# A decoder block on one core: forty transfers that add up weight blocks in memory, issued from a_v to projection B instead of in the FFN input stage

## The chip, the cores and the metric

The kernel is one launch on one core of a Trainium2 chip. The metric is the device time of that launch in microseconds (us), shown as the median of several runs. The engines named below are PE (matrix multiply; PEld is its weight load), DVE (vector), ACT (scalar), POOL and SP. SP computes nothing here: it issues most of the DMA transfers. POOL computes a little, and it issues the transfers that add to memory. Each engine works through its instructions in the order of the program. An instruction that waits holds up everything behind it on the same engine.

## The reference, cut to what matters

One layer of a decoder for 512 positions of 1024 channels in float32, followed by a final norm:

```python
h = rms_norm(x, norm1_g) * (1.0 + scale1) + shift1          # scale, shift, gate from silu(c) @ w_ada
z = h @ w_in                                                # a_u | a_v | q | k | v | qi | ki | wi | g_a | g_b
y_a = chunked_gmlp(gelu(a_u), gelu(a_v), ...)
y_b = dsa_attention(q, k, v, qi, ki, wi)                    # top-256 keys by an indexer score
merged = sigmoid(g_a) * (y_a @ w_proj_a) + sigmoid(g_b) * (y_b @ w_proj_b)
x = x + gate1 * (merged @ w_out)
h2 = rms_norm(x, norm2_g) * (1.0 + scale2) + shift2
f_g, f_u = split(h2 @ w_ffn_in)
x = x + gate2 * ((silu(f_g) * f_u) @ w_ffn_out)
return rms_norm(x, final_norm_g)
```

`w_ffn_out` has 2816 x 1024 elements. `w_ada` has 1024 x 6144 elements; its six sections of 1024 columns give shift1, scale1, gate1, shift2, scale2 and gate2.

## The kernel before, in words

**Products.** Each float32 operand is split into a rounded part `hi` and a rest `lo`, and a product is three matmuls: hi x hi, hi x lo, lo x hi (`mm3`, lines 53 to 55). ACT makes `hi` of a weight chunk (line 112). DVE or POOL makes `lo` (line 116).

**Stages.** In the order of the program: the norm and the adaLN numbers; q, k, v and the indexer; a_v (8 weight chunks); a_u (8 chunks); then four times one group of gate A and one of projection A (16 chunks); attention with the gate B products mixed in (19 rounds); projection B (8 chunks); the output projection; the FFN input stage (20 rounds, lines 1590 to 1700, tile `R`); the FFN output stage (tile `pfo`); the final norm.

**Block sums.** The output projection, the FFN input and the FFN output use a Strassen-like scheme: seven products of half-size blocks instead of eight. The weight side of the FFN output needs sums of blocks of `w_ffn_out`. Four such sums, `wsum1` to `wsum4`, are formed in DRAM by DMA alone, five chunks of 256 x 512 elements (512 KB) each. One chunk takes six steps (`wsum_steps`, lines 292 to 314): two copies into wsum1 and wsum3; two accumulating transfers on top of them; a copy wsum1 to wsum2; an accumulation on wsum2; a copy wsum2 to wsum4; an accumulation on wsum4. Plain copies are issued by SP (line 307), accumulating ones by POOL (line 305). That is 20 copies and 20 accumulations. Each step has to wait until the transfers of the chunk's step before it have landed, and the engine that issues it does the waiting. The sums are first read in the FFN output stage (`raw<-wsum`).

**Where the steps stand before.** `wstep()` issues the next step of a list. It is called twice in each of the 20 rounds of the FFN input stage. In the list the chunks 0 and 1 alternate, then 2 and 3; chunk 4 comes last, with an empty entry after each step.

**The other loads of SP.** Weight chunks `raw` (512 KB) go into three rotating buffers. A load is issued in program order by `ensure`, when `room` allows it, and SP then waits until the buffer's last reader is done. Loads of `w_ada` for the later sections ("mods", `mod_sec`, lines 200 to 228) stand in the same list: in the gate A and projection A groups one mod follows each weight chunk. Such a load goes into a single buffer `mraw` (line 205), and DVE adds its rows, times the silu of c, onto `acc` (lines 175 and 177). As there is one buffer, the next `mraw` load is issued only when that sum is done, and the weight load that follows it in the list is issued behind it. Sections 2, 3 and 4 are formed so from the end of a_u to projection B, 24 loads of 512 KB, of which 16 belong to the gate A and projection A groups. Section 5 is formed in rounds 1 to 8 of the FFN input stage (`last_mod`), two loads at a time.

**DVE beside it.** From a_v to the end of projection A DVE also runs the top-k search of the indexer (lines 709 and 713), the mixing of a_u (lines 920 and 922) and the products of projection A with its gate (line 995). At the start of attention it makes `lo` of the first gate B chunks (line 116) and the first softmax (line 1029).

**Names in the code around the change.** `opt_b` runs a group of chunks and calls `post` after each of them; `au_post` is that `post` in a_u, gate A and projection A; the loop over `s in range(NU + 3)` is attention; `o_step` is called once in each chunk of projection B.

Of the kernel before, what the change touches and what calls it, by code (L numbers as in the profile page):

```python
# [28 lines left out]
def block_kernel(ctx: ExitStack, tc: tile.TileContext, x, positions, w_ada, b_ada, w_in,  # L29
# [15 lines left out]
    def f(ap):  # L45
        return ap.bitcast(F32)
# [72 lines left out]
    def ensure(upto):  # L119
        upto = min(upto, len(stream) - 1, st["limit"] - 1)  # L120
        while True:
            for i in range(st["prep"], min(st["prep"] + 16, len(stream), st["limit"])):
                if "raw" in stream[i]:
                    continue
                if room(i):
                    issue(i)
                elif stream[i]["kind"] == "w" or not stream[i]["mid"]:
                    break
            if st["prep"] > upto:
                break  # L130
            prep(st["prep"])
            st["prep"] += 1
# [11 lines left out]
    def get(i, ahead=2):  # L144
        k = wseq.index(i)
        ensure(wseq[min(k + ahead, len(wseq) - 1)])
        return chunk[i]
# [144 lines left out]
    def wsum_steps():  # L292

        def step(c, *moves):
            o = slice(256 * c, 256 * c + 256)

            def fn():
                for n, add, src in moves:
                    if isinstance(src, tuple):
                        k = KZ[src[0]][2 * c] * 128  # L300
                        src = w_ffn_out[k:k + 256, 512 * src[1]:512 * src[1] + 512]
                    else:
                        src = wsum[src][o]
                    if add:
                        P.dma_start(wsum[n][o], src, accum_op=OP.add)  # L305
                    else:
                        SY.dma_start(wsum[n][o], src)
            return fn

        parts = [[step(c, *m) for m in (  # L310
            ((1, 0, (0, 0)), (3, 0, (0, 1))), ((1, 1, (0, 1)), (3, 1, (1, 1))), ((2, 0, 1),), ((2, 1, (1, 1)),),
            ((4, 0, 2),), ((4, 1, (1, 0)),))] for c in range(NZ)]
        return ([fn for c in (0, 2) for two in zip(parts[c], parts[c + 1]) for fn in two] +
                [fn for one in parts[4] for fn in (one, None)])

    wsteps = wsum_steps()

    def wstep():
        fn = wsteps.pop(0) if wsteps else None
        if fn:  # L320
            fn()
    assert next(mm_, None) is None
    sec_done = []
    tick = [0]
# [549 lines left out]
    for g in range(4):  # L874
        pb = [bank2(b, "pav") for b in nbanks()]
        for i in W_AV[g]:
            for fn in VT.get(vs, []):
                fn()
            if iu[1] < 24:
                idx_accs()  # L880
            else:
                run_bg(2.0)
            if vs % 2 == 0 and vs:
                for tk in range(4):
                    V.bn_stats(bst[:, tk, (g - 1) * 6:g * 6], vg[tk // 2][:, tk % 2, (g - 1) * 256:g * 256])
            vs += 1
            hi, lo = get(i)
            for tk in range(4):
                opt_a_mm(pb[tk // 2][:, tk % 2], tk, hi, lo, stream[i]["kts"], hT, 8, tk % 2 == 0)
            idx_mms(3)  # L890
        for b in range(2):
            A.activation(vg[b][:, :, g * 256:(g + 1) * 256], pb[b], AF.Gelu_apprx_tanh)
# [34 lines left out]
    AT = {3: [0], 4: [1, 2], 5: [3], 6: [4], 7: [5], 8: [6], 9: [7]}  # L927

    def au_post():
        for m in AT.get(austep[1], []):  # L930
            mix_mm(m)
        austep[1] += 1
# [152 lines left out]
    def gb_part(n, ahead=2):  # L1085
        for k in range(gbn[0], min(gbn[0] + n, 32)):
            g, kt = divmod(k, 8)
            i = W_GB[g][kt // 4]
            hi, lo = get(i, ahead)
            if k % 2 == 0:  # L1090
                mbank[0] = (7, 1, 0, 7)[g]
                sec_tasks()
            if kt == 0:
                gbp[g] = [bank(b, "pgb") for b in ((0, 1), (7, 0), (1, 7), (0, 1))[g]]
            for m in range(2):
                cc = slice(m * 128, (m + 1) * 128)
                mm3(gbp[g][m], (hi[:, kt % 4, cc], lo[:, kt % 4, cc]), hT[kt], kt == 0, kt == 7)
            if kt == 7:
                for m in range(2):
                    A.activation(gbt[g][:, m], gbp[g][m], AF.Copy)  # L1100
        gbn[0] += n
# [4 lines left out]
    for s in range(NU + 3):  # L1106
        if s >= 3:
            yh, yl, pp = at_pv(s - 3)
            A.activation(yh, pp, AF.Copy)
            V.tensor_sub(yl, pp, f(yh))  # L1110
        if s < NU:
            at_qk(s)
            at_soft_a(s)
            if s == 0:
                pa_last[0]()
                at_split(2)
        if 2 <= s <= NU + 1:
            for o, ol, p in at_T(s - 2):
                A.activation(o, p, AF.Copy)
                V.tensor_sub(ol, p, f(o))  # L1120
        if 1 <= s <= NU:
            at_soft_b(s - 1)
        if s < NU:
            at_exp(s)
        if 0 < s < NU - 2:
            at_split(s + 2)
        gb_part(GBN[s], 2 if s else 1)
    mbank[0] = 6

    for g in range(4):  # L1130
# [73 lines left out]
    def o_step():  # L1204
        for fn in O_STEPS.pop(0):
            fn()

    mbank[0] = 5
    o_issue("B11", "B12", "B22")
# [3 lines left out]
    sec_tasks(True)  # L1213


    ss2 = base.tile([128, 4, 5], F32, name="ss2")
    V.memset(ss2, 0.0)
    V.memset(ss2[:, :, 4:5], EPS)
# [404 lines left out]
    for q in range(-2, NQ):  # L1623
        g, u = 2 + q // 2, q % 2
        d = sd[q]
        s_issue(q + 2)
        pre = s_prep(q + 1)
        half_of = lambda t, e: tuple(v[:, :, e] for v in t)
        S2_, S1_, A12, A22, S4_, S3_ = (half_of(d[k], e) for k in "CBD" for e in range(2))
        R = [bank(k, "R")[:, :256] for k in ((4, 1, 0, 7), (5, 2, 3, 6))[q % 2]]  # L1630
        ps = [ffn[0].tile([128, 256], F32, name="ps", tag="rt", bufs=2) for _ in range(2)]
        if q == NQ - 2:
            for i in W_Z[0, 0][:2]:
                issue(i)
        t0, t1 = slice(0, 256), slice(256, 512)
        if u:
            dst = [gtile(2 * g + m) for m in range(2)]
        else:
            fs[0], fs[1] = t512("fs"), t512("fs")
            dst = fs  # L1640
        cur = dict(fs)

        def out_direct(m, p, u=u, dst=dict(enumerate([dst[0], dst[1]])), cur=cur):
            if u:
                V.tensor_mul(dst[m][:, t0], cur[m][:, t0], p)
            else:
                A.activation(dst[m][:, t0], p, AF.Silu)

        def out_late(m, u=u, dst=dict(enumerate([dst[0], dst[1]])), cur=cur):
            if u:  # L1650
                V.tensor_mul(dst[m][:, t1], dst[m][:, t1], cur[m][:, t1])
            else:
                A.activation(dst[m][:, t1], dst[m][:, t1], AF.Silu)

        pre[0][0]()
        sprod(R[0], d["A"], HB[0, 0], True)
        A.activation(R[1], R[0], AF.Copy)  # L1657
        for fn in pre[0][1:]:
            fn()
        while left:  # L1660
            left.pop(0)()
        if q == NQ - 1:
            issue(W_Z[0, 0][2])
        sprod(R[3], S1_, TB[1], True)
        A.activation(ps[0], R[3], AF.Copy)
        for fn in pre[1]:
            fn()
        sprod(R[1], S2_, TB[2], False)
        wstep()
        A.activation(R[2], R[1], AF.Copy)  # L1670
        pre[2][0]()
        pre[2][1]()
        sprod(R[0], A12, HB[1, 0], False)
        if not u:
            out_direct(0, R[0])
        sprod(R[2], S3_, TB[3], False)
        A.activation(ps[1], R[2], AF.Copy)
        pre[3][0]()
        pre[3][1]()
        if u:  # L1680
            out_direct(0, R[0])
        V.tensor_add(dst[1][:, t1], R[3], ps[1])
        sprod(R[1], S4_, HB[1, 1], False)
        out_late(1)
        V.tensor_add(dst[0][:, t1], R[1], ps[0])
        sprod(R[2], A22, TB[4], False)
        out_late(0)
        left.append(lambda fn=out_direct, p=R[2]: fn(1, p))
        if 1 <= q <= 8:
            last_mod(q - 1)  # L1690
        if q == 9:
            last_gate()
        if q == 10:
            for b_ in (3, 2):
                mbank[0] = b_
                sec_tasks(one=True)
        wstep()
        if q in (9, 13, NQ - 2):
            a_sum("S1", {9: 0, 13: 2}.get(q, 1))
    assert not wsteps  # L1700


    xo = []
# [134 lines left out]
    for tk in range(2):  # L1838
        for z in range(2) if tk else (None,):
            c = ALL if z is None else slice(256 * z, 256 * z + 256)  # L1840
# [66 lines left out]
```

## Time and profile before

| | |
|---|---|
| median of 3 runs | 831.74 us (831.45 to 832.74) |
| the profiled execution | 831.31 us |
| its span from first to last instruction | 829.5 us |
| FFN input stage in it (505 to 711 us) | 206 us |
| first and last copy of the block sums issued | 497.8 and 671.0 us |
| first and last accumulation issued | 506.8 and 677.3 us |
| first load of a finished block sum | 711.1 us |

The profile shows one execution. Times on its axis start at the first instruction. A row of the timeline has the start, the duration, the engine, the line and what is written and read; brackets give the idle time just before it and what ended it. A row of the stage view has, after the stretch and its length, the busy time of PE, PEld, DVE, ACT and POOL with the number of instructions, then the granted clock of PE (1.00 is full), the busy share of the 16 DMA engines, and GB/s. For DMA, "to landing" is the time from the issue until the data has arrived.

### The profile page before, as it was taken

How to read it: one execution, taken by the hardware profiler on the slowest of the kernel's cores; microseconds unless marked ns; L12 is line 12 of the kernel's file. 1: busy time of each engine (PE TensorE's matmuls, PEld its weight loads, DVE VectorE, ACT ScalarE, POOL GpSimd, SP SyncE). 2: the span in 40 equal slices, each digit the busy share in tenths (PEclk: the TensorE clock that was granted, in tenths of full speed). 3: DMA queues.
4: the chain of work that ended last, by engine and by line, in shares of the span. 5: the costliest groups of instructions: out<-in, count | busy, mean ns of one | idle time of the engine just before them, and what ended most of it. 6: DMA issues, size and time to landing. Idle time of an engine off the chain costs nothing.

```text
span 829.5 us, 12872 instructions
## 1 busy us (share of the span) xinstructions
PE 810.3 (98%) x4920; PEld 723.6 (87%) x4920; DVE 684.5 (83%) x1167; ACT 427.0 (51%) x730; POOL 126.7 (15%) x121
## 2 busy tenths in 40 slices
PE   7999999999999999999999999999899999999995
PEld 6889889988888888988888899999899999888784
DVE  7989788798899558886697869899699888897676
ACT  6674444323322236665536586555355556666543
POOL 2060032362353411000000001001000000000001
PEclk9999999999999999999999999999999999999999
DMA  9974352423345652057531409899998863556533
GB/s 296 310 203 118 102 178 77 118 87 101 124 137 176 197 178 77 26 157 243 185 102 50 154 28 257 222 271 295 254 265 208 199 162 125 178 189 195 177 129 126
DMA packets 108477, 138.46 MB, mean 167 GB/s; under 512 B 6480, under 2 KB 77136, under 8 KB 108256
## 3 DMA queue, kind: packets, MB, share of 16 engines
q1 hardware_dynamic: 99872, 120.24, 45.7%
q0 software_dynamic: 7824, 16.59, 10.4%
q8 instruction: 38, 0.62, 0.3%
q10 hardware_dynamic: 720, 0.82, 0.3%
q14 instruction: 23, 0.19, 0.1%
HBM read 135.26 MB, written 23.07 MB: 191 GB/s over the span
## 4 chain that ended last, share of the span: by engine, by line
PE 50%; DVE 18%; DMA 6%; ACT 2%; issue 2%; POOL 0%; POOLq 0%; ACTq 0%; DVEq 0%
PE R L53 6%; PE R L54 6%; PE R L55 6%; DMA mraw<-in_w_ada_dram 6%; PE pfo L55 3%; PE pfo L53 3%; PE pfo L54 3%; DVE acc L177 3%; DVE sco L713 2%; DVE m L709 2%; PE pb L53 2%; PE pb L55 2%; PE pb L54 2%; DVE lo L116 2%; PE po L54 2%
## 5 line engine op out<-in xcount | busy, mean ns | idle before, releaser
L112 ACT ACTIVATE hi<-raw 128x1024 fp32r<-128x1024 f32 (+2 forms) x103 | 107.0, 1040 | 105.3 <-PE pfo L55 34.3
L116 DVE TENSOR_TENSOR lo<-raw,hi 128x1024 fp32r<-128x1024 f32 (+2 forms) x67 | 81.1, 1214 | 29.1 <-ACT hi L112 28.9
L116 POOL TENSOR_TENSOR lo<-raw,hi 128x1024 fp32r<-128x1024 f32 x29 | 73.3, 2531 | 127.9 <-ACT hi L112 122.2
L53 PE MATMUL pb<-h,hi 128*128 128x512 f32 (+1 forms) x192 | 74.6, 389 | 0.0
L54 PE MATMUL pb<-h,hi 128*128 128x512 f32 (+1 forms) x192 | 74.0, 385 | 0.0
L55 PE MATMUL pb<-h,lo 128*128 128x512 f32 (+1 forms) x192 | 74.0, 385 | 0.0
L54 PE MATMUL pfo<-lo,za 128*128 128x512 f32 (+1 forms) x146 | 56.3, 385 | 0.3 <-DVE lo L116 0.3
L55 PE MATMUL pfo<-hi,za 128*128 128x512 f32 (+1 forms) x146 | 56.2, 385 | 0.0
L53 PE MATMUL pfo<-hi,za 128*128 128x512 f32 (+1 forms) x146 | 56.1, 385 | 0.0
L177 DVE SCALAR_TENSOR_TENSOR acc<-mraw,cols,acc 128x512 f32<-128x512 f32 x49 | 39.6, 808 | 18.9 <-DMA mraw<-in_w_ada_dram 17.9
L53 PE MATMUL R<-tb,hi 128*128 128x256 f32 x160 | 45.0, 281 | 2.9 <-ACT R L1670 2.1
L53 PE MATMUL R<-tb,sx 128*128 128x256 f32 x160 | 45.3, 283 | 0.9 <-ACT R L1657 0.8
L54 PE MATMUL R<-tb,sx 128*128 128x256 f32 x160 | 45.1, 282 | 0.0
L55 PE MATMUL R<-tb,sx 128*128 128x256 f32 x160 | 45.0, 281 | 0.0
L55 PE MATMUL R<-tb,lo 128*128 128x256 f32 x160 | 44.9, 281 | 0.0
L54 PE MATMUL R<-tb,hi 128*128 128x256 f32 x160 | 44.7, 279 | 0.0
L305 POOL DMA_DIRECT2D wsum<-in_w_ffn_out_dram x20 | 17.8, 908 | 172.7 <-DMA wsum<-wsum 115.3
L55 PEld LDWEIGHTS pb<-h,lo 128*128 128x128 f32 x192 | 36.0, 187 | 7.3
L54 PEld LDWEIGHTS pb<-h,hi 128*128 128x128 f32 x192 | 36.0, 188 | 6.9
L53 PEld LDWEIGHTS pb<-h,hi 128*128 128x128 f32 x192 | 36.0, 188 | 6.9
L1235 POOL TENSOR_TENSOR sm<-sm,mhalf 128x1 f32<-128x1 f32 x8 | 5.3, 662 | 217.6 <-DVE sm L1234 217.6
L54 PE MATMUL pav<-lo,h 128*128 128x256 f32 x128 | 35.8, 279 | 0.0
(373 smaller groups left out, 2643.6 us busy)
## 6 DMA issues: line engine op xcount, KB each, us to landing
raw<-in_w_ffn_in_dram SPq DMA_DIRECT2D x44, 512.0 KB, 6.5
raw<-in_w_in_dram SPq DMA_DIRECT2D x40, 512.0 KB, 3.8
mraw<-in_w_ada_dram SPq DMA_DIRECT2D x28, 512.0 KB, 4.0
wsum<-in_w_ffn_out_dram POOLq DMA_DIRECT2D x20, 512.0 KB, 9.3
raw<-wsum SPq DMA_DIRECT2D x20, 512.0 KB, 3.7
raw<-in_w_ffn_out_dram SPq DMA_DIRECT2D x18, 512.0 KB, 3.8
s<-in_w_ada_dram SPq DMA_DIRECT2D x30, 256.0 KB, 5.6
wsum<-in_w_ffn_out_dram SPq DMA_DIRECT2D x10, 512.0 KB, 8.6
```

What stands on the lines that cost most here:

```text
L53: T.matmul(o, wh, rh, start=start, stop=False, **kw)
L54: T.matmul(o, wh, rlo, start=False, stop=False, **kw)
L55: T.matmul(o, wlo, rh, start=False, stop=stop, **kw)
L112: A.activation(hi[:, :m], e["raw"][:, :m], AF.Copy)
L116: e["lo"].tensor_sub(lo[:, :m], e["raw"][:, :m], f(hi[:, :m]))
L177: V.scalar_tensor_tensor(o, w, cs[:, j:j + 1], o, op0=OP.mult, op1=OP.add)
L305: P.dma_start(wsum[n][o], src, accum_op=OP.add)
L709: V.max(m8s[i], sco[i])
L713: V.match_replace(out=sco[i], in_to_replace=m8s[i], in_values=sco[i], imm_value=TAKEN)
L1235: P.tensor_tensor(r2[:, tk:tk + 1], r2[:, tk:tk + 1], mhalf[:, :1], op=OP.pow)
```

## The change

The steps themselves, their order for the chunks 0 to 3 and their sizes stay as they are. The calls of `wstep()` move: once per chunk of a_v (8 calls), in `au_post` (24 calls), once per round of attention (19), in `o_step` (8), 59 calls in all, of which every second one issues a step. The 30 steps are thus spread over 29 calls, and the last one is issued after projection B. The empty entries behind the steps of chunk 4 go. The FFN input stage issues none.

```diff
-        return ([fn for c in (0, 2) for two in zip(parts[c], parts[c + 1]) for fn in two] +
-                [fn for one in parts[4] for fn in (one, None)])
+        return [fn for c in (0, 2) for two in zip(parts[c], parts[c + 1]) for fn in two] + parts[4]
 
     wsteps = wsum_steps()
+    wcount = [0]
 
     def wstep():
-        fn = wsteps.pop(0) if wsteps else None
-        if fn:
-            fn()
+        wcount[0] += 1
+        if wsteps and wcount[0] % 2 == 0:
+            wsteps.pop(0)()
...
             hi, lo = get(i)
+            wstep()
             for tk in range(4):
                 opt_a_mm(pb[tk // 2][:, tk % 2], tk, hi, lo, stream[i]["kts"], hT, 8, tk % 2 == 0)
...
     def au_post():
+        wstep()
         for m in AT.get(austep[1], []):
             mix_mm(m)
...
         gb_part(GBN[s], 2 if s else 1)
+        wstep()
...
         for fn in O_STEPS.pop(0):
             fn()
+        wstep()
...
     sec_tasks(True)
 
 
+    for fn in wsteps:
+        fn()
...
         sprod(R[1], S2_, TB[2], False)
-        wstep()
         A.activation(R[2], R[1], AF.Copy)
...
-        wstep()
         if q in (9, 13, NQ - 2):
             a_sum("S1", {9: 0, 13: 2}.get(q, 1))
-    assert not wsteps
```

## The prediction, made before the changed kernel had run

> **What bounds the kernel now.** First the page, for the engines and the DMA queues:
>
> ```profile
> span 829.5 us, 12872 instructions
> PE 810.3 (98%) x4920; PEld 723.6 (87%) x4920; DVE 684.5 (83%) x1167; ACT 427.0 (51%) x730; POOL 126.7 (15%) x121
> q1 hardware_dynamic: 99872, 120.24, 45.7%
> q0 software_dynamic: 7824, 16.59, 10.4%
> ```
>
> PE is the bound, so a change can only give back or create idle time of PE. Then the view by stages (a_v; a_u; gate A and projection A in two parts; attention; projection B; FFN input), where the last three numbers are the granted clock, the DMA share and GB/s:
>
> ```profile
> 104.00:168.00 64.00, 64.00 (x478) 61.29 (x477) 53.05 (x93) 27.66 (x46) 19.55 (x19) 1.00 0.41 124
> 168.00:215.00 47.00, 47.00 (x227) 38.74 (x226) 43.07 (x70) 14.26 (x20) 22.65 (x9) 1.00 0.30 90
> 215.00:240.00 25.00, 25.00 (x121) 20.74 (x120) 22.66 (x46) 9.06 (x12) 9.79 (x5) 1.00 0.40 127
> 240.00:307.00 67.00, 67.00 (x294) 54.37 (x293) 46.73 (x105) 16.06 (x20) 24.85 (x10) 1.00 0.60 188
> 307.00:392.00 85.00, 84.73 (x497) 74.11 (x496) 70.48 (x205) 52.34 (x133) 4.62 (x5) 1.00 0.39 122
> 392.00:437.00 45.00, 45.00 (x201) 36.87 (x200) 36.31 (x48) 19.71 (x24) 0.00 (x0) 1.00 0.45 145
> 505.00:711.00 206.00, 202.16 (x1684) 201.09 (x1683) 179.54 (x242) 115.70 (x204) 18.37 (x21) 0.99 0.83 221
> ```
>
> The stages that receive the transfers show no idle PE to speak of; the FFN input stage, which loses them, has 3.8 us of it, at a DMA share of 0.83. Where it idles, from the waits of PE and DVE there and three equal stretches:
>
> ```profile
> PE R L53 <- ACT R L1670: 2.1, 1, 2.1
> DVE acc L175 <- DMA mraw<-in_w_ada_dram: 6.4, 1, 6.4
> 574.00:589.00 15.00, 15.00 (x129) 15.00 (x129) 11.31 (x17) 7.23 (x14) 2.65 (x3) 1.00 1.05 213
> 589.00:604.00 15.00, 11.31 (x80) 10.61 (x79) 11.37 (x16) 6.85 (x13) 1.76 (x2) 0.89 0.88 248
> 604.00:619.00 15.00, 15.00 (x129) 15.00 (x128) 14.13 (x20) 8.04 (x14) 0.87 (x1) 1.00 0.99 318
> 593.50:597.00 3.50, 3.08 (x16) 2.78 (x14) 3.47 (x6) 1.27 (x3) 0.00 (x0) 0.51 1.18 453
> 576.81 1.19 SPq L205 DMA_DIRECT2D mraw<-in_w_ada_dram  x2
> 592.49 0.49 DVE L175 TENSOR_SCALAR acc<-mraw,cols 128x512 f32<-128x512 f32 x1 [6.37 <-DMA mraw<-in_w_ada_dram]
> ```
>
> A load of `w_ada` issued at 576.81 was there at 592.5. DVE stood 6.4 us for it, PE ran dry, and after that PE had half its clock for 3.5 us. The middle stretch did 80 matmuls, its neighbours 129.
>
> **Part 1: the FFN input stage is freed.** The 49 missing matmuls at 15/129 = 0.116 us each are 5.7 us. How late such a load is with and without the transfers beside it (landing of `mraw` from 213 to 307 us, then from 500 to 640 us):
>
> ```profile
> DMA to landing us min/median/max: 3.7/3.9/4.2
> DMA to landing us min/median/max: 8.6/10.3/16.6
> ```
>
> DVE wanted the load at 592.49 - 6.37 = 586.1, so 9.3 us after its issue. Two loads at once without the transfers should need about 6 (4.2 and one more load of 1.65, below). Nothing else is late next, so I take the whole gain: **-5.7 us**. The bounds are 0 (the wait stays) and -5.7.
>
> **Part 2: issuing.** Every copy and accumulation is still issued once, elsewhere:
>
> ```profile
> L305 POOL DMA_DIRECT2D wsum<-in_w_ffn_out_dram x20: 872/881/1307, 506.8 to 677.3; - x20
> L307 SPq DMA_DIRECT2D wsum<-in_w_ffn_out_dram x10: 505/602/1172, 497.8 to 630.8; - x10
> L307 SPq DMA_DIRECT2D wsum<-wsum x10: 473/522/3041, 524.9 to 671.0; - x10
> ```
>
> SP: 20 x 0.6 = 12 us. In the new places the weight and `mraw` loads queue behind, but SP stands some 4 us per chunk there until a load has landed, so 0.5 to 1.2 us per call is hidden. POOL: 20 x 0.88 = 17.6 us. Behind it queue the `lo` subtractions; POOL is busy 24.85 of 67 us in its densest stage, so this is hidden too. Without these covers a call would cost up to 0.6 us (SP) or 0.9 us (POOL) per transfer. As to waiting: with two chunks in turn, a chunk's next step comes four calls later, over 20 us, and the transfers land in 5.5 to 10.7 us (copies) and 6.6 to 14.9 us (accumulations):
>
> ```profile
> DMA to landing us min/median/max: 5.5/8.2/10.7
> DMA to landing us min/median/max: 6.6/9.3/14.9
> ```
>
> Only chunk 4, alone in projection B with two calls (about 11 us) between its steps, can hold SP, by up to 14.9 - 11 = 4 us, with projection B's loads queued behind. I take 0 and keep 4 for the range.
>
> **Part 3: the DMA load goes where a chain of loads sets the pace.** By the page, q1 takes 45.7% of 829.5 us for 120.24 MB, 3.15 us per MB, so 1.65 us per 512 KB. q0 has 86.3 us for 16.59 MB. The 20 accumulations are 10.5 MB of that; the other 6.1 MB are plain loads of POOL, 19 us at q1's rate, which leaves 67 us, 3.4 us per accumulation. By calls, a_v gets 4 copies and 4 accumulations, a_u 2 and 2, gate A and projection A 6 and 6, attention 6 and 4, projection B 2 and 3, one accumulation comes after. From 215 to 307 us the DMA engines are busy 0.40 x 25 + 0.60 x 67 = 50 us of 92 now; 6 x 1.65 + 6 x 3.4 = 30 us come on top, 80 of 92. Attention and projection B go to some 90 of 130.
>
> That would fit if nobody waited. But in gate A and projection A a loop runs (SP issues, DVE sums, SP issues the next):
>
> ```profile
> 251.04 0.37 SPq L205 DMA_DIRECT2D mraw<-in_w_ada_dram  x1
> 255.02 1.64 DVE L177 SCALAR_TENSOR_TENSOR acc<-mraw,cols,acc 128x512 f32<-128x512 f32 x2 [0.44 <-DMA mraw<-in_w_ada_dram]
> 256.69 0.37 SPq L205 DMA_DIRECT2D mraw<-in_w_ada_dram  x1
> 305.30 1.54 DVE L177 SCALAR_TENSOR_TENSOR acc<-mraw,cols,acc 128x512 f32<-128x512 f32 x2 [4.00 <-DMA mraw<-in_w_ada_dram]
> 306.76 2.35 DVE L116 TENSOR_TENSOR lo<-raw,hi 128x1024 fp32r<-128x1024 f32 x2
> 309.14 0.48 PE L53 MATMUL pgb<-h,hi 128*128 128x512 f32 x1
> ```
>
> Issue, 3.9 us to landing, 1.5 us of sum, the next issue: 5.6 us, and ten rounds of it in a row from 251 to 307 us. Any delay of one landing moves all that follows. The loop ends in front of the `lo` of the first gate B chunk (306.76 to 307.95), which PE uses at 309.14: 1.2 us of slack, and behind it PE is busy 84.73 of 85 us, so nothing is made up.
>
> What each load in the loop meets (pairs of accumulations beside `mraw` are what the 8.6 and 10.3 us above had: +4.7 to +6.4 per pair, so +2.4 to +3.2 for one, I take 2.8):
> - last chunk of a_u, one accumulation: the load issued at 216.69 is there at 220.6 and used at 222.28, which hides 1.7 to 1.9. It costs 0.9 (0 to 1.5).
> - groups 1, one accumulation each, at about 249 and 260 us, when POOL is through with its `lo`: the load of 251.04 meets the first in full, 2.8 (2 to 3.4); the second meets the following loads in part, 1.4 (0 to 3.2).
> - groups 2, two copies each, in SP's own queue right behind a weight load: 2 x 1.65 = 3.3 us against 5.5 - 2 x 1.65 = 2.2 free per round: 1.1 each, 2.2 (1 to 5).
> - groups 3, two accumulations each, free to go once group 2's copies have landed, some 8 us after their issue: four of them for the last two loads. 0 if they come after the last load; 2 x 6.4 = 12.8 if each load meets a pair; the load at 576.81, beside four, had +12.7. I take 8, as the copies land before the last two loads go.
>
> The rows for the first:
>
> ```profile
> 216.69 0.37 SPq L205 DMA_DIRECT2D mraw<-in_w_ada_dram  x1
> 222.28 1.52 DVE L177 SCALAR_TENSOR_TENSOR acc<-mraw,cols,acc 128x512 f32<-128x512 f32 x2
> ```
>
> Sum of the lag: 0.9 + 2.8 + 1.4 + 2.2 + 8 = 15.3 us (3 to 25.9). Less 1.2 of slack: **+14.1 us** of PE idle, nearly all at the start of attention.
>
> By the Trainium skill (DMA: Bandwidth & Descriptors, "Queues, rings and completion order") a DMA engine takes turns between its queues packet by packet, so a load of SP's queue is not held by all that POOL has queued, only by about as many packets as it has itself. By that rule the last two loads cost at most one accumulation each, 6.8 instead of 8, and the sum below is 1.2 us lower; the row with +12.7 beside four speaks for more, so I keep 8.
>
> **Part 4: PE's clock after the idle.** After the stall in the FFN stage the clock was 0.51 for 3.5 us, with 16 matmuls where 30 fit: 14 x 0.116 = 1.6 us. The same price after the new, longer stall: **+1.6 us** (0 to 3.2, for two stalls).
>
> The Trainium skill (TensorE: Matmul & The Clock Gate, "Part 1: The HAM clock gate") has the half clock set in after an idle window of about 3.4 us. Here a stall of 2.1 us was enough. By the rule, a stall cut into pieces shorter than that would cost nothing here, and the sum would be 1.6 us lower; I go by the row.
>
> **Sum.** Against the profiled execution, 831.3 us (1.8 outside its span; the median of the runs is 0.4 higher): 831.3 - 5.7 + 14.1 + 1.6 = **841.3 us**.
>
> **The rivals.**
> - *The loop gets by, and the gain stays (the other side).* The place is the same loop; the price of its lag decides. If the accumulations fall between the loads, as a DMA share of 0.60 leaves room for, the lag stays within its slack of 1.2 us and the time is 831.3 - 5.7 = 825.6. With the low end of the lag, 3 us, it is 825.6 + 1.8 = 827.4. At 1.2 + 5.7 = 6.9 us of lag the gain is used up; beyond that it is slower. For it: 80 of 92 us is not full. Against: four accumulations need 13.6 us within the last two rounds of 5.6.
> - *Nothing to tell.* Lag of 5.3 to 8.6 us: 829.7 to 833.
> - *The change does not free the FFN stage:* the wait at 592 us stays, as two `w_ada` loads still go out at once with the weight loads. Then 841.3 + 5.7 = 847. Against: without the transfers no `mraw` took over 4.2 us.
> - *More is lost behind:* attention and projection B get 7 accumulations, and chunk 4 holds SP. The 4 us of part 2, and the upper end of the lag (25.9 instead of 15.3, +10.6): 841.3 + 10.6 = 852, at most 856.
>
> **How the numbers follow.** Slower by the loop, 834 to 850: 0.55. The FFN stage not freed: 0.05. More lost, over 850: 0.08. About the same: 0.07. The loop gets by: 0.25. What a measurement of this kernel can tell from no change is 0.2%, 1.7 us. So faster 0.25, same 0.07, slower 0.68. The prediction is 841.3; alone, its case goes from 834 to 850. The range for all is 827 to 852, leaving out some of the cases at either end.
>
> **What would show it.** Right: from 505 to 711 us the clock is 1.00 throughout, no wait of `acc` for `mraw`, about 200 us for the stage; in gate A and projection A landings of `mraw` of 6 to 10 us and larger waits of DVE for them; `lo` of the first gate B chunk about 14 us later against projection A's end, with PE idle before `pgb` and half its clock after. Wrong: landings there under 5 us, or a DVE lag that PE does not see; or PE idle in attention or projection B on `raw` loads instead.

## The result, and the profile after

The changed kernel takes 849.82 us (median of 4 runs, 849.71 to 850.53), against 831.6 for the kernel before in the same runs: a ratio of 1.0219 with an interval of 1.0201 to 1.0236. That is 18.2 us slower. The forecast was 841.3 (827 to 852): the direction holds, and the net loss is 18 us where 10 were forecast.

The page of the changed kernel, engines and queues:

```profile
span 847.9 us, 12865 instructions
PE 812.9 (96%) x4920; PEld 724.7 (85%) x4920; DVE 689.0 (81%) x1167; ACT 425.8 (50%) x730; POOL 125.8 (15%) x121
q1 hardware_dynamic: 99872, 120.24, 44.2%
q0 software_dynamic: 7824, 16.59, 9.7%
```

The work is the same: 4920 matmuls, and both queues move the same bytes as before. PE fell from 98% to 96% of a longer span. Three landmarks of PE in both traces say in which part of the program the time went (first matmul of gate B, of the FFN input stage and of the FFN output stage; us):

| | first `pgb` | first `R` | first `pfo` | span |
|---|---|---|---|---|
| before | 309.1 | 504.6 | 710.9 | 829.5 |
| after | 329.6 | 528.8 | 729.3 | 847.9 |
| later by | 20.5 | 24.2 | 18.4 | 18.4 |

So 20.5 us were lost up to the start of attention, 3.7 more up to the FFN input stage, and 5.8 came back in it. The stages of the changed kernel, cut where they now lie (a_v; the two parts of gate A and projection A; the gap; the first matmuls of gate B; attention; projection B; FFN input):

```profile
104.00:168.00 64.00, 64.00 (x479) 61.27 (x478) 53.05 (x92) 27.73 (x46) 23.09 (x23) 1.00 0.63 178
215.00:240.00 25.00, 25.00 (x122) 20.77 (x121) 21.64 (x45) 8.94 (x12) 10.71 (x6) 1.00 0.58 169
240.00:313.00 73.00, 69.55 (x300) 55.40 (x299) 48.93 (x101) 14.97 (x19) 29.48 (x16) 1.00 0.69 203
313.00:329.60 16.60, 1.24 (x7) 0.83 (x6) 3.87 (x5) 2.64 (x3) 0.50 (x1) 0.64 0.91 214
329.60:335.00 5.40, 5.40 (x15) 4.30 (x14) 5.33 (x13) 1.52 (x4) 0.00 (x0) 0.53 0.63 191
335.00:414.00 79.00, 79.00 (x472) 69.87 (x472) 64.48 (x193) 49.13 (x127) 8.03 (x9) 1.00 0.58 167
414.00:459.00 45.00, 45.00 (x201) 36.85 (x200) 33.28 (x44) 19.52 (x24) 3.56 (x4) 1.00 0.80 234
523.30:729.40 206.10, 205.95 (x1733) 205.57 (x1732) 185.29 (x251) 120.62 (x215) 0.54 (x1) 1.00 0.40 129
```

The reader is to see three things. The FFN input stage has lost its idle time, its clock is 1.00, and its DMA share fell from 0.83 to 0.40. The stages a_v and projection B took the transfers without idle time of PE in this trace, at DMA shares of 0.63 and 0.80. And in front of gate B there is a gap of 16.6 us with 7 matmuls. What PE waited for, over the whole span (total, times, longest; the waits at the start and the end of the program are left out):

```profile
PE mod L436 <- DVE acc L177: 15.4, 1, 15.4
...
PE mod L430 <- DVE ah L220: 2.2, 1, 2.2
PE pb L53 <- DVE part L997: 0.9, 1, 0.9
...
PE po L53 <- ACT po L1368: 0.7, 1, 0.7
```

Behind the first three (at 328.9, 270.5 and 278.2 us) stands the same engine, DVE, which is late by its sums of `mraw`. What DVE waited for from 213 to 330 us, and how long `mraw` took to land there; then how long it took from 500 to 640 us:

```profile
DVE acc L177 <- DMA mraw<-in_w_ada_dram: 29.0, 9, 8.7
DVE acc L175 <- DMA mraw<-in_w_ada_dram: 8.2, 2, 6.1
DMA to landing us min/median/max: 3.4/3.8/9.8
...
DMA to landing us min/median/max: 4.7/6.1/7.0
```

The median in the gates is 3.8 us, where it was 3.9, but six of the fifteen loads take 6.1 to 9.8. In the FFN input stage it is the other way: 4.7 to 7.0, where it was 8.6 to 16.6. The end of the loop in the timeline:

```profile
307.26 0.37 SPq L205 DMA_DIRECT2D mraw<-in_w_ada_dram  x1
317.05 1.54 DVE L177 SCALAR_TENSOR_TENSOR acc<-mraw,cols,acc 128x512 f32<-128x512 f32 x2 [8.68 <-DMA mraw<-in_w_ada_dram]
318.61 0.37 SPq L205 DMA_DIRECT2D mraw<-in_w_ada_dram  x1
327.20 1.54 DVE L177 SCALAR_TENSOR_TENSOR acc<-mraw,cols,acc 128x512 f32<-128x512 f32 x2 [8.62 <-DMA mraw<-in_w_ada_dram]
328.66 2.36 DVE L116 TENSOR_TENSOR lo<-raw,hi 128x1024 fp32r<-128x1024 f32 x2
328.89 1.09 PE L436 MATMUL mod<-cst,acc 128*128 128x128 f32 x4 [15.36 <-DVE acc L177]
329.63 0.78 PE L53 MATMUL pgb<-h,hi 128*128 128x512 f32 x1
```

The rounds that took 5.6 us before take 11.4 and 10.1 here: DVE stands 8.7 and 8.6 us for the last two loads, does nothing else meanwhile, and PE stands for DVE.

**The lag, load by load.** SP issues 15 `mraw` loads in this stretch, and the same 15 can be found in both traces. The lag is how much later the next load is issued (for the last one: when the sum is done, 328.74 against 306.84).

| load issued (before, after) | lag grows by | what is beside it |
|---|---|---|
| 216.69, 216.78 | 1.2 | the accumulation of a_u; landing 6.7 |
| 240.08, 241.33 | 4.1 | no transfer; a DVE instruction that lasts 2.5, then one of 2.8 |
| 245.43, 250.75 | 3.0 | first accumulation of the groups; landing 7.1 |
| 262.19, 270.02 | 2.0 | second accumulation; landing 6.2 |
| 267.68, 277.51 | 0.8 | no late transfer; a sum held up by POOL again |
| 285.14, 294.73 | 2.0 | two copies; landing 6.1 |
| 296.02, 307.26 | 6.0 | two copies issued at 303.06 and 303.62, in flight for 7.8 and 8.5; accumulations issued from 305.84 on; landing 9.8 |
| 301.33, 318.61 | 4.6 | the rest of the four accumulations; landing 8.5 |
| all others | -1.9 | of which -0.8 because a sum that POOL held up before no longer meets a `lo` |

The sum with the 0.1 at the start is 21.9 us; less the 1.4 of slack that was used up (306.84 to 309.14 before, 328.74 to 329.63 now), 20.5, which is the first landmark.

The second row is not a matter of DMA. DVE and POOL in the timeline around it:

```profile
241.34 2.50 DVE L220 CAST ah<-acc 128x512 fp32r<-128x512 f32 x1
247.96 2.76 DVE L177 SCALAR_TENSOR_TENSOR acc<-mraw,cols,acc 128x512 f32<-128x512 f32 x1
...
240.68 2.87 POOL L116 TENSOR_TENSOR lo<-raw,hi 128x1024 fp32r<-128x1024 f32 x1 [0.71 <-ACT hi L112]
247.64 2.54 POOL L116 TENSOR_TENSOR lo<-raw,hi 128x1024 fp32r<-128x1024 f32 x1 [4.08 <-ACT hi L112]
```

The cast takes 0.43 us in the trace before and the sum 0.75 as a rule. Here both begin just after a `lo` of POOL has begun, and end 0.3 and 0.5 us after that `lo` has ended. The a_u delay of 1.2 us had shifted DVE against POOL.

The clock at the gap, in four stretches:

```profile
314.00:317.60 3.60, 0.00 (x0) 0.00 (x0) 0.55 (x1) 0.00 (x0) 0.00 (x0) 1.00 1.09 228
317.60:329.60 12.00, 0.71 (x4) 0.74 (x5) 3.31 (x5) 2.64 (x3) 0.00 (x0) 0.50 0.84 208
329.60:334.70 5.10, 5.10 (x14) 4.04 (x13) 5.03 (x13) 1.52 (x4) 0.00 (x0) 0.50 0.65 197
334.70:340.00 5.30, 5.30 (x28) 4.42 (x28) 3.79 (x11) 3.15 (x7) 0.00 (x0) 1.00 0.03 10
```

Half clock holds for 17.1 us, but PE has hardly any work before the last 5.1 of them: 14 matmuls there, where the next 5.3 us do 28. That is half of 5.1 us, about 2.5.

### The profile page after: what moved, and what is told of

It reads as the page before. It is cut to its first block, busy times and chain, and to the rows that moved or that the text cites. A ratio compares the mean times of both kernels' runs of the same rounds, so it can differ in the third digit from the quotient of the medians.

```text
span 847.9 us, 12865 instructions
## 1 busy us (share of the span) xinstructions
PE 812.9 (96%) x4920; PEld 724.7 (85%) x4920; DVE 689.0 (81%) x1167; ACT 425.8 (50%) x730; POOL 125.8 (15%) x121
## 4 chain that ended last, share of the span: by engine, by line
PE 48%; DVE 17%; DMA 8%; ACT 4%; issue 2%; POOL 0%; POOLq 0%; DVEq 0%
PE R L53 8%; PE R L54 7%; PE R L55 7%; DMA mraw<-in_w_ada_dram 7%; PE pfo L55 3%; PE pfo L54 3%; PE pfo L53 3%; DVE acc L177 3%; PE pgb L53 2%; PE pgb L54 2%; PE pgb L55 2%; DVE sco L713 2%; DVE m L709 2%; DVE lo L116 1%; DVE vg L902 1%
## 5 line engine op out<-in xcount | busy, mean ns | idle before, releaser
L177 DVE SCALAR_TENSOR_TENSOR acc<-mraw,cols,acc 128x512 f32<-128x512 f32 x49 | 41.5, 848 | 35.6 <-DMA mraw<-in_w_ada_dram 34.6
L53 PE MATMUL pav<-hi,h 128*128 128x256 f32 x128 | 35.8, 280 | 0.0
L55 PE MATMUL pav<-hi,h 128*128 128x256 f32 x128 | 35.8, 280 | 0.0
```

Source lines behind the costliest of these rows:

```text
L53: T.matmul(o, wh, rh, start=start, stop=False, **kw)
L55: T.matmul(o, wlo, rh, start=False, stop=stop, **kw)
L177: V.scalar_tensor_tensor(o, w, cs[:, j:j + 1], o, op0=OP.mult, op1=OP.add)
```

## The experiments

The theory after this reading: the accumulating transfers, by their time on the DMA engines, hold up a loop that has one buffer, in the gates now and in the FFN input stage before. The rivals: it is the copies or the issuing and waiting of SP and POOL that costs; the lag of DVE comes from POOL and not from DMA; the FFN input stage gained for another reason. "Thin" below means that an accumulating transfer adds 16 rows of a block instead of 256: it is issued, waited for and queued as ever, but moves a sixteenth of the data.

**No transfers in the gates.** All steps that fell in gate A and projection A go to the end of the list and into the FFN input stage.

```diff
     def au_post():
-        wstep()
+        if austep[1] < 8:
+            wstep()
...
+        if q >= 9:
+            wstep()
+            wstep()
```

> The changed kernel, but no step is issued in gate A and projection A: a_v and a_u issue 8 of the 30 steps, attention and projection B 13, and the last 9 go, one per round, into rounds 9 to 17 of the FFN input stage, where no load of w_ada is left. All 40 transfers are made. Theory (the loop of mraw loads in gate A and projection A pays for the transfers): the loop runs as before, landings of mraw back at 3.7 to 4.2 us, no stall before the first gate B product, and the FFN stage keeps its 5.7 us: 826 us (824 to 829). Rival (the transfers cost wherever they stand beside weight loads): only the share of the 8 steps out of 30 goes, about 843 us.

Measured: 832.21 us (ratio 1.0011, 0.9996 to 1.0025). The waits of PE, without the ones at the start:

```profile
PE pv L54 <- DVE tl L1123: 1.7, 2, 1.0
...
PE pb L55 <- DVE lo L116: 1.6, 1, 1.6
PE po L53 <- ACT po L1367: 0.8, 1, 0.8
```

The gap is gone (first `pgb` at 309.9), and so is the stall of the FFN input stage (200.5 us from first `R` to first `pfo`). But the expected 826 was missed: from first `pgb` to first `R` it takes 202.2 us instead of 195.5, in small stalls of attention and projection B. The 849.8 of the changed kernel hide most of this: there the same stretch takes 199.2, of which some 2.5 are the half clock.

**The same, with the accumulations behind the gates thin.**

```diff
+        thin[0] = True
         wstep()
...
     sec_tasks(True)
+    thin[0] = False
...
-                        P.dma_start(wsum[n][o], src, accum_op=OP.add)
+                        r = 16 if thin[0] else 256
+                        P.dma_start(wsum[n][256 * c:256 * c + r], src[:r], accum_op=OP.add)
```

> The kernel with quiet gates (no step in gate A and projection A), and the accumulations issued in attention and projection B add 16 rows instead of 256, which leaves out most of these additions; their issue, the waits and the copies stay. It asks where the 6 us went that the quiet gates did not give back. Theory: the accumulations' time on the DMA engines delays loads there too: 826 to 828 us. Rival (copies in SP's queue, SP or POOL waiting for steps to land): 831 us or more.

Measured: 826.43 us (0.9946, 0.9931 to 0.9961). The stretch from `pgb` to `R` is 196.3 us. Attention and projection B, in the run without and then in the run with thin accumulations:

```profile
307.00:392.00 85.00, 82.95 (x486) 72.11 (x485) 71.33 (x204) 50.84 (x130) 9.79 (x11) 1.00 0.63 165
392.00:440.00 48.00, 46.40 (x206) 37.51 (x205) 32.47 (x44) 19.54 (x25) 1.82 (x2) 1.00 0.79 253
```

```profile
307.00:392.00 85.00, 83.99 (x493) 73.39 (x492) 70.59 (x205) 52.23 (x133) 9.07 (x11) 1.00 0.49 162
392.00:440.00 48.00, 48.00 (x214) 39.26 (x213) 39.12 (x53) 21.23 (x27) 1.59 (x2) 1.00 0.51 169
```

The 5.8 us are thus the DMA time of the accumulations in these two stages: the copies and all issues were still there. A thin transfer also lands sooner, so a wait for it would be shorter; but in the run without thin ones SP stood for no step, since each of its copies there goes out right behind the load issued before it (at 403.93, for one, behind a load at 403.47). The DMA share fell from 0.63 to 0.49 in the one and from 0.79 to 0.51 in the other.

**The accumulations of the gates thin; and only the last four of them.** The two runs differ in the bound, 8 or 20; all copies stay whole.

```diff
     def au_post():
+        thin[0] = austep[1] >= 8
         wstep()
+        thin[0] = False
```

> The changed kernel, but the 6 accumulations issued in gate A and projection A add 16 rows instead of 256; every issue, wait and copy stays. This leaves out most of these additions. Theory (what delays the loop is the time that the accumulations take of the DMA engines, 17 of the 22 us of lag): the lag falls to some 5 us, the stall before gate B to 0 to 4 us, 826 to 831 us. Rival (issue and waits on POOL and SP, or the 6 copies): the stall stays, 843 us or more.

> The changed kernel, but only the last 4 accumulations of that stage (after the last chunks of gate A and projection A) add 16 rows instead of 256, which leaves out most of these four additions. Theory: they hold the last two mraw loads by 5.9 and 4.6 us, 10.5 together; without them PE waits that much less, and 1 to 2.5 us of half clock go too: 836.5 to 839 us. Rival (the lag comes from the earlier steps, and the last loads would be late anyway): 846 us or more.

Measured: 834.25 us with all six thin (1.0041, 1.0025 to 1.0057) and 842.01 with the last four thin (1.0122, 1.0102 to 1.0142). The longest wait of PE, in the first and then in the second:

```profile
PE mod L438 <- DVE acc L177: 3.7, 1, 3.7
```

```profile
PE mod L438 <- DVE acc L177: 7.9, 1, 7.9
313.38 1.54 DVE L177 SCALAR_TENSOR_TENSOR acc<-mraw,cols,acc 128x512 f32<-128x512 f32 x2 [6.04 <-DMA mraw<-in_w_ada_dram]
```

So the six cost 15.6 us of the time, the last four 7.8 of that, and the gap shrinks from 15.4 to 7.9 to 3.7. The second number missed its expected range by some 3 us, and the row under the second wait shows why. The last load came down to 3.7 us, but the load before it, issued at 306.24, still took 7.1, beside the two whole copies issued at 302.0; so PE's wait fell by 7.5 us where 10.5 were expected. From the issue of the first of these two loads to the end of the last sum it takes 10.8 us before the change, 21.5 after it and 14.0 here: of the 10.7 us of lag in that place the four accumulations account for 7.5, and 3.2 remain without them, which points at the copies. What the shorter half clock gave back, small stalls behind took again (1.8 at `pv`, 1.5 at `pb`), as in the run with quiet gates. The 834.25 of the first run lie over the expected range for the same reasons: the copies and the a_u accumulation (which was whole) are in the 3.7, and from first `pgb` to first `R` it takes 199.2 us where it took 195.5 before.

**The kernel before, all its 20 accumulations thin.** One line, `thin = [True]`, with the transfers where they were.

> The kernel before, with its 20 accumulations, in their old place in the FFN input stage, cut to 16 rows of 256, so most of the additions are left out; the 20 copies stay whole. Theory (the stall at 592 us comes from the time that the accumulations take of the DMA engines): the stall and the half clock behind it go, 5.7 us: 826 us. Rival (two w_ada loads issued together with the weight loads are late by themselves): 831 us as before.

Measured: 825.43 us against 830.95 of the kernel before beside it (0.9922, 0.9908 to 0.9937). The stage from 505 to 711 us, and the landing of `mraw` from 500 to 640:

```profile
505.00:711.00 206.00, 205.85 (x1706) 204.25 (x1706) 183.54 (x248) 117.84 (x207) 15.96 (x21) 1.00 0.56 177
...
DMA to landing us min/median/max: 4.0/5.9/7.0
```

All that the FFN input stage had to give is 5.5 us, and it is the DMA time of the accumulations that took it, not the 20 copies, which were whole.

**Two buffers for `mraw`.** From the sixth load of the groups on, loads go in turn into two buffers, so that one can be issued while the one before is in flight or being summed. All transfers stay in place.

```diff
-            raw = mid.tile([128, 1024], F32, name="mraw", tag=e["mid"], bufs=1)
+            raw = mid.tile([128, 1024], F32, name="mraw", tag=mtag(i), bufs=1)
...
+        if e["kind"] == "m" and e["mid"] == "A2" and mtag(i) != mtag(i, -1):
+            return sum(p["kind"] == "m" for p in pend) <= 1 and len(pend) <= 3
```

> The changed kernel, but from the sixth load on the mraw loads of gate A and projection A alternate between two buffers, and a load may be issued while the one before it has not been summed. All transfers stay where the change put them. Theory (each late landing is paid because the loop is one load deep): most of the lag is hidden, DVE's waits for mraw there fall from 37 us to under 12, the stall before gate B from 15 us to under 5; 833 to 839 us, as some 6 us are lost in attention and projection B too. Rival (the DMA engines are full in that stage, whatever the depth): 846 us or more.

Measured: 829.63 us (0.9979, 0.9956 to 1.0002), which is below the expected range. DVE's wait for `mraw`, and the longest wait of PE:

```profile
DVE acc L186 <- DMA mraw<-in_w_ada_dram: 8.6, 3, 4.2
...
PE qk L53 <- DVE mx L1040: 3.1, 1, 3.1
```

With the same transfers beside them, the loads still take up to 8.4 us to land, but DVE waits 8.6 us in all instead of 37.2. So 20 us of the changed kernel's time hang on the depth of the loop, not on the DMA engines being full. The ten executions spread from 826.2 to 833.9 us. The profiled one took 833.7, and there the expected loss behind the gates is present: 201.7 us from first `pgb` to first `R`. What the shorter executions save, and where the 3.1 at the start of attention comes from, stays open.

**`lo` of two chunks on DVE instead of POOL.** This is the rival that POOL holds DVE up.

```diff
+    for i_ in W_PA[1]:
+        stream[i_]["lo"] = V
```

> The changed kernel, but DVE instead of POOL makes lo of the two weight chunks of the second projection A group. Theory of the 4 us that the lag gained at 241 and 248 us with no late load (the cast to ah took 2.50 us and a sum on acc 2.76, beside POOL's lo, and both ended with it): these two go back to 0.43 and 0.75 us, for two lo of 1.22 us more on DVE; the time changes by -3 to +1 us. Rival (they are slow by the transfers in flight): they stay at 2.5 us or more.

Measured: 848.32 us (one run), 1.5 less than the changed kernel and inside the expected -3 to +1. The waits of PE:

```profile
PE mod L438 <- DVE acc L177: 10.6, 1, 10.6
PE pb L55 <- DVE lo L116: 5.3, 1, 5.3
```

The long cast and the long sum at 241 and 248 us are gone. In their place PE waits 5.3 us for the `lo` that DVE now makes, and the two waits together, 15.9 us, are as long as the one they replace (15.4). So that POOL's `lo` holds these instructions of DVE up is confirmed, but its worth in time stays open: no run here takes it away without putting a new wait in its place.

**Other places.** Twelve steps (chunks 0 and 1) go to 15 calls of a_v and a_u, three out of four, and the other 18 to the FFN input stage, one per round. Gates, attention and projection B get none.

```diff
-        if wsteps and wcount[0] % 2 == 0:
+        if wcount[0] < 16 and wcount[0] % 4:
             wsteps.pop(0)()
...
+        if wsteps:
+            wsteps.pop(0)()
         if q in (9, 13, NQ - 2):
```

> All 40 transfers, none in gate A, projection A, attention or projection B: the 12 steps of chunks 0 and 1 in calls 1 to 15 of a_v and a_u (three of every four calls), the 18 steps of chunks 2 to 4 in the FFN input stage, one per round, so that no more than two accumulations stand beside its w_ada loads. Theory: neither the loop nor the FFN stage stalls; 826 us (824.5 to 828.5), faster than both kernels. Rivals: the denser a_v and a_u delay DVE there and the loop after it: 830 us or more; or the FFN stall comes back: 831 us.

Measured: 825.11 us (ratio to the kernel before 0.9929, 0.9916 to 0.9943), 6.7 us faster than the kernel before beside it (831.84) and 24.7 than the change. Three stretches (a_v and a_u, gates, FFN input), and the landing of `mraw` in the gates:

```profile
104.00:215.00 111.00, 111.00 (x705) 100.11 (x704) 96.08 (x162) 42.11 (x65) 48.09 (x35) 1.00 0.68 185
215.00:307.00 92.00, 92.00 (x410) 75.00 (x409) 69.99 (x148) 24.78 (x30) 34.21 (x14) 1.00 0.53 172
503.80:704.20 200.40, 200.25 (x1685) 199.88 (x1684) 179.91 (x243) 115.14 (x204) 11.21 (x13) 1.00 0.67 186
...
DMA to landing us min/median/max: 3.4/3.7/4.3
```

PE never idles in them. A_v and a_u have a DMA share of 0.68 without loss (one load of `mraw` alone falls into them, at 195.9), and the FFN input stage copes with 18 steps instead of 30. No wait of PE between the start-up and the FFN output stage remains.

## Why the prediction was right or wrong

| step | predicted | measured |
|---|---|---|
| Part 1, FFN input stage | -5.7 | -5.8 by landmarks; -5.5 with thin accumulations before |
| Part 2, issuing and SP's waits | 0 | none seen |
| Part 3, a_u accumulation | 0.9 | 1.2 |
| groups 1, two accumulations | 4.2 | 5.0 |
| groups 2, two copies each | 2.2 | 2.0 for the first two; the other two in the next row |
| groups 3, four accumulations | 8 | 10.7, of which 3.2 remain with the four thin |
| DVE held up by POOL | not in it | 4.9 |
| regained | 0 | -1.9 |
| slack | -1.2 | -1.4 |
| Part 4, half clock | 1.6 | about 2.5 |
| stalls behind the gap | 0 | 1.2 (3.7 less the clock) |
| sum | +10.0 | +18.4 |

**Part 1** held in size, and in its cause: with the accumulations thin the stall is gone. One link in it was read wrongly, that DVE stood for `mraw` and so "PE ran dry". PE's longest wait there, 2.1 us, ended at 592.18, before DVE had its load at 592.49. It ended with ACT, which had stood for a weight load of the FFN stage (rows of the kernel before):

```profile
590.80 1.06 ACT L1335 ACTIVATE sx<-raw 128x1024 fp32r<-128x1024 f32 x1 [3.06 <-DMA raw<-in_w_ffn_in_dram]
591.76 0.37 ACT L1670 ACTIVATE R<-R 128x256 f32<-128x256 f32 x1
```

Only the two waits of 0.8 us behind it came through DVE and `mraw`. So weight loads were late beside the accumulations too.

**Part 2** held. No wait of PE leads to SP or POOL issuing, and the run with thin accumulations behind the gates, with every issue in place, shows none of the price. Chunk 4 did not hold SP up: in the changed kernel its later copies go out at 437.16 and 451.38, right behind the weight loads issued at 436.70 and 450.96.

**Part 3** had the mechanism and the place right: a one-buffer loop in front of gate B. Its lag came to 21.9 us where 15.3 were forecast, inside the range of 3 to 25.9. Two terms failed. One is that of the copies, "1.1 each, 2.2": it set each pair against the free DMA time of one round of 5.5 us, but the copies were in flight for 7.5 to 8.5 us. The first two cost 2.0; the other two were still moving beside the first of the last two loads, and 3.2 us of lag remain there when the accumulations are thin. That makes some 5.2, just over the upper bound of 5. The term of the four accumulations, "I take 8", comes to 7.5 by the same run; that they would meet the last two loads was right. The other failed term was missing altogether: the sum counted a DVE sum of 1.5 us per round, although the trace of before has a pair of sums that takes 3.52 us instead of 1.5 (at 236.53, beside a `lo` of POOL), and a loop that is shifted meets other `lo`. That is 4.9 us, less 0.8 for a meeting that no longer takes place. The small terms held to within 1 us.

The price of one accumulation, 2.8, agrees with what single ones cost here (landings of 6.2, 6.7 and 7.1 for 3.8), but that is luck. It compared loads that are issued two at a time, at 8.6 us (least) and 10.3 (median), with single loads at 3.9. The same pairs of loads without the transfers land in 4.7 and 6.1 us in the changed kernel, and with that the comparison gives about 2.

By the Trainium skill (DMA: Bandwidth & Descriptors, "Queues, rings and completion order") the last two loads should have cost 6.8 at most, one accumulation each. The trace has 10.7: the landings of 9.76 and 8.50 are 5.9 and 4.6 over the 3.9 of an undisturbed load. The part of the accumulations, 7.5, is over that bound too. But the bound counted only the load's own packets. While the first of the two loads was on its way (307.26 to 317.02 us), the queues of POOL (q0) and SP (q1) moved:

```profile
q0 software_dynamic: 488, 0.96, 57.1%
q1 hardware_dynamic: 783, 1.41, 48.3%
```

SP's queue also held the rest of the two copies, and it moved more packets than POOL's. So these rows don't speak against the rule, as far as the packets that the profile counts are those of the rule; they speak against the bound as I had worked it out. A packet of POOL's queue held a DMA engine for 0.18 us and one of SP's for 0.10 (the shares of 16 engines over 9.76 us, divided by the packets).

**Part 4** was of the right kind, with 2.5 for 1.6. The rule of the Trainium skill's clock page (TensorE: Matmul & The Clock Gate, "Part 1: The HAM clock gate") agrees with the gap: the records show half clock from 317.6 us, some 4 us after PE's last matmul (begun at 313.14), for an idle window of about 3.4. My reading that 2.1 us are enough doesn't hold in general: the 2.2 us stall of this trace, in the stretch from 240 to 313 us, left the clock there at 1.00. Why the stall of 2.1 us in the kernel before was followed by half clock stays open.

**The rivals.** "The loop gets by" and "nothing to tell" fell with the gap; "the FFN stage is not freed" fell with its 200.5 us. "More is lost behind" is half true: the upper part of the lag came, 6.6 of the 10.6 it allowed; SP's 4 us did not. The stages behind the gap would themselves cost 5.8 us, as the quiet gates show, by the DMA time of the accumulations, not by SP's wait that this rival named. In the changed kernel little of that appears (1.2). A likely reason, not tested, is that the weight loads get ahead while PE stands.

## What to carry to other kernels

Before moving transfers into a stage with free DMA time, look for a loop there that issues a load only after the last one was used: once its slack is used up, every microsecond a load is late is a microsecond of lag, at a mean DMA share of 0.69 as much as at 0.9. Count every transfer that is still in flight when such a load is issued, those of its own queue too. Either give the loop a second buffer (849.8 to 829.6 us here) or put the transfers where loads are issued well ahead of use (825.1). And free slots are not all alike: sum the DMA time that a transfer takes, not its bytes, and look at what the delay brings together on the other engines.

## What the runs showed of the hardware

An accumulating transfer in memory costs about twice a plain load of the same size in DMA time (3.4 against 1.65 us per 512 KB, from the queues' rows). It also adds to the landing time of a load beside it: one adds 2.4 to 3.3 us (landings of 6.2, 6.7 and 7.1 for a median of 3.8).

A `lo` subtraction on POOL of 2.4 us can hold a DVE instruction until it ends: 2.50 instead of 0.43, 2.76 instead of 0.75. The Trainium skill (GPSIMD Engine Reference, "Key points") states that the two engines share their SBUF interfaces and names instructions with two SBUF inputs among those that collide. The trace agrees for the sum, whose row has two such inputs, `mraw` and `acc`; the cast reads one tensor, so this does not speak of it. The trace adds the size: both instructions end 0.3 to 0.5 us after POOL's, which looks like standing until the other is through rather than like running slower.

Half clock lasts on past the end of a stall: after 15.4 us of idle PE, another 5.1 us of work at half speed. In the clock records of these traces, between the start-up and the end of the program, it comes in stretches of 3.41 us (kernel before), 6.83 (last four thin), 13.65 (`lo` on DVE) and 17.07 (changed kernel): one, two, four and five times the same length.
